# A joint opening of three weight groups in layer 1, and first token differences made in mid-layer

## The chip, the cores and the metric

The kernel runs on one core of one Trainium2 chip. The metric is the device time of one execution in microseconds (us). Three runs of the kernel before took 1093.97, 1093.69 and 1090.76 us: the median is 1093.69 us.

A core has a matrix engine (TensorE, PE in the profile), whose weight loads are listed apart (PEld), and three engines for elementwise work: VectorE (DVE), ScalarE (ACT) and GpSimd (POOL). SyncE (SP) issues the DMAs. Each engine works through its own queue in order, and semaphores make one wait for another.

## The reference

The reference is a block of two layers over 1024 latent tokens of width 1024. Layer 0 mixes tokens by a Fourier transform in half of its channels and by differential attention in the other half. Layer 1 is a short gated convolution. Only layer 1 matters here, and of it this is what is computed:

```python
h = rms_norm(x, g) * (1.0 + scale) + shift
bg, cg, xt, g = jnp.split(h @ odd_w_in, 4, axis=-1)      # 1024 x 4096
u = cg * xt
up = jnp.pad(u, ((0, 0), (1, 1), (0, 0)))
conv = sum(conv_w[t] * up[:, t:t + n] for t in range(3))
y = (bg * conv * jax.nn.silu(g)) @ odd_w_out             # 1024 x 1024
return x + gate * y
```

All is float32.

## The kernel before, in words

Features lie on the 128 partitions, tokens along the free axis, in two halves of 512 (NB). A float32 product is made of three matmuls of a faster 32-bit format: each operand is split into a high part (a cast on ACT) and a low part (the operand less its high part, a subtract on DVE or POOL), and high x high, high x low and low x high are added in PSUM.

**Seven products for eight.** Layer 1's two projections are done in 20 *groups*: 16 for the input projection (0 to 15) and 4 for the output projection (16 to 19). A group has two column tiles of 128 features, and its 2 x 2 blocks (token half by input half) are computed with seven products instead of eight, from sums and differences of blocks. A product (g, p), p = 1 to 7, is 4 quarters of 3 matmuls, each 128x128 by 128x512, in `quarters`. It needs a weight operand, made by `wop` and `wpart` from the raw tiles `wraw` of its group, and a token operand B[p] of four tiles (k = 0 to 3), each with a high and a low part. The token operands are shared by all groups of a projection: B[1] and B[2] are parts of the first token half, B[5], B[6], B[7] and B[4] are differences (t1, t2, t3, t4 in the code), and B[3] is a part of the second half. Each difference is formed from the one before it. The weight operand of p = 5 takes three or four elementwise steps on POOL (L634), the others none.

Products 1, 6, 7 and 4 of a group add into one PSUM bank, X, without starting anew. Between them ACT or DVE must read the bank, and the next product waits for that. Product 2 uses bank Z, products 5 and 3 use bank Y. `finish1` does the elementwise work behind each product of groups 0 to 15: even groups give u = cg * xt and end with the convolution (`conv`, two scalings on ACT and 12 taps on DVE, L1389, result in `vv`), odd groups give bg * silu(g) and are multiplied by `vv`; their results are listed in `ysd`. `finish2` does the output projection's.

**The opening of layer 1.** While layer 0's output projection of the second token half still runs (`out0(1, f)`), the first half is normalised and B[1] and B[2] are made. What needs the second half waits for its norm: token sums (`stats1`, small matmuls in mid-product), rs and dg on DVE with a power on POOL between, then a broadcast matmul (`ps_rows`), whose result `scaled` reads. TensorE does meanwhile the products that need the first half alone: (0,1), (0,2), (1,1), (1,2), with the token sums in the middle of (0,2) and the broadcast in the middle of (1,1). Then groups 0 and 1 go on together through p = 5, 6, 7, while B[5], B[6], B[7], B[4], B[3] are made just ahead of them, and (0,4), (0,3) close the opening. Group 2 begins behind it. In this part the order of every engine's queue is the program's (a manual schedule of PE, DVE, ACT and POOL). The low parts of B alternate between DVE and POOL, as do those of the weights.

**The middle**, up to group 14, fixes TensorE's order alone; a planner with costs of its own orders the other engines. Weights are prepared five products ahead (LEAD). Weight operands go round six buffers, in the pools `wp` (4) and `w2` (2); raw tiles have two buffers in each pool, and a group's are reloaded when product 3 of the group two before it has been prepared.

**The end**, from (14,1) on, is again in program order on all four engines. Here a weight's high part is cast at one product and its low part made behind the next (the lists `rests` and `due`). The token operands of the output projection are made from `ysd` by `bop`, at the places listed in `hooks`: a subtract where B is a difference, a cast, and a low part that is held back by one step (`lows`).

## Time and profile before

| | |
|---|---|
| median of three runs | 1093.69 us |
| the profiled execution | 1093.98 us |
| its span | 1092.2 us |
| TensorE busy | 1039.5 us (95%) |
| DVE busy | 753.0 us (69%) |
| ACT busy | 481.9 us (44%) |
| POOL busy | 466.8 us (43%) |
| mean granted TensorE clock | 0.981 |

A row of the timeline gives the start and the duration of an instruction in us, its engine, the line of the kernel, what it writes and reads, and in brackets how long the engine had been idle and what ended that. "xN" stands for N instructions merged. The durations of matmuls overlap: it is the distance of their starts that tells their rate. The granted clock is 1.00 where TensorE runs at full speed.

### The profile page before, as it was taken

Reading aid. Unit: us, or ns where it says so; the run is one execution under the profiler, and the core shown is the slowest. Engines: PE = TensorE matmul, PEld = TensorE weight load, DVE = VectorE, ACT = ScalarE, POOL = GpSimd, SP = SyncE. Lnnn points to the kernel's source line nnn. Section 1 sums busy time; section 2 is a strip of 40 time slices with the busy share of each in tenths; the row PEclk is TensorE's granted clock in tenths of the full one; section 3 lists DMA queues with packets and bytes.
Section 4 is the critical chain, followed back from the end, with each engine's and each line's share of the span. In section 5 each row is a group of like instructions: output and inputs, shape, how many; then the busy total and the mean of one; then the engine's idle time right before and its main releaser. Section 6 shows DMA issues by size and latency. Waiting matters only on the chain.

```text
span 1092.2 us, 14128 instructions
## 1 busy us (share of the span) xinstructions
PE 1039.5 (95%) x5128; PEld 847.3 (78%) x5128; DVE 753.0 (69%) x1093; ACT 481.9 (44%) x876; POOL 466.8 (43%) x398
## 2 busy tenths in 40 slices
PE   6989999999999899999999998899999999998998
PEld 3667888878877698999888886578888888786786
DVE  4599956958786388888853287986545645578953
ACT  4453333313345377777753363633333333344420
POOL 1257115620445147766575445655344354402041
PEclk8999999999999999999999999999999999999999
DMA  9823895353112978161006450121111211202431
GB/s 337 329 97 113 260 367 214 110 166 115 59 44 78 244 185 189 38 163 57 11 20 210 166 189 34 38 77 40 59 58 39 77 40 58 77 20 97 143 126 59
DMA packets 61381, 131.12 MB, mean 120 GB/s; under 512 B 5248, under 2 KB 30208, under 8 KB 58112
## 3 DMA queue, kind: packets, MB, share of 16 engines
q1 hardware_dynamic: 60240, 125.64, 36.7%
q0 software_dynamic: 1072, 4.59, 1.2%
q8 instruction: 40, 0.66, 0.2%
q14 instruction: 29, 0.24, 0.1%
HBM read 105.57 MB, written 24.64 MB: 119 GB/s over the span
## 4 chain that ended last, share of the span: by engine, by line
PE 64%; DVE 20%; POOL 5%; ACT 4%; issue 3%; DMA 3%; SPq 0%; ACTq 0%; POOLq 0%; DVEq 0%
PE psX L657 6%; PE psX L659 6%; PE psX L658 6%; PE ps_av L1075 5%; PE ps_tok L284 3%; PE ps_tok L285 3%; PE ps_tok L286 3%; PE psY L657 3%; PE psY L659 3%; PE psY L658 3%; PE S L1025 3%; PE S L1026 2%; DVE nm L1030 2%; PE ps_t L1065 2%; PE ps_feat L1128 2%
## 5 line engine op out<-in xcount | busy, mean ns | idle before, releaser
L284 PE MATMUL ps_tok<-whi,hhi 128*128 128x512 f32 x288 | 118.5, 412 | 2.5 <-ACT hhi L393 1.5
L285 PE MATMUL ps_tok<-whi,hlo 128*128 128x512 f32 x288 | 115.3, 400 | 3.6 <-DVE hlo L397 3.5
L286 PE MATMUL ps_tok<-wlo,hhi 128*128 128x512 f32 x288 | 114.6, 398 | 0.0
L61 ACT CAST wop<-wraw 128x512 fp32r<-128x512 f32 x118 | 72.5, 620 | 93.4 <-PE ps_feat L1130 27.6
L1030 DVE TENSOR_REDUCE nm<-S 128x1 f32<-128x1280 f32 x64 | 95.2, 1487 | 20.5 <-PE S L1026 18.4
L634 POOL TENSOR_TENSOR s<-wraw 128x512 f32<-128x512 f32 x20 | 27.9, 1395 | 185.3 <-DMA wraw<-in_wodd_dram 118.1
L62 POOL TENSOR_TENSOR wop<-wraw,wop 128x512 fp32r<-128x512 f32 x60 | 83.1, 1388 | 51.5 <-ACT wop L61 51.5
L1041 ACT ACTIVATE p<-S,nm 128x1280 f32<-128x1280 f32 x64 | 85.1, 1330 | 43.2 <-DVE nm L1030 39.4
L657 PE MATMUL psX<-B,wop 128*128 128x512 f32 x240 | 96.7, 403 | 7.5 <-ACT c L1363 3.5
L658 PE MATMUL psX<-B,wop 128*128 128x512 f32 x240 | 96.5, 402 | 1.5 <-POOL B L1510 1.0
L659 PE MATMUL psX<-B,wop 128*128 128x512 f32 x240 | 96.1, 401 | 1.8 <-DVE wop L1310 1.3
L1075 PE MATMUL ps_av<-v,aT 128*128 128x128 f32 x640 | 76.8, 275 | 0.0
L1075 PEld LDWEIGHTS ps_av<-v,aT 128*128 128x128 f32 x640 | 74.2, 192 | 0.2
L285 PEld LDWEIGHTS ps_tok<-whi,hlo 128*128 128x128 f32 x288 | 55.5, 193 | 16.9 <-DVE hlo L397 6.0
L659 PE MATMUL psY<-B,wop 128*128 128x512 f32 x160 | 64.3, 402 | 4.1 <-DVE wop L1310 4.1
L284 PEld LDWEIGHTS ps_tok<-whi,hhi 128*128 128x128 f32 x288 | 55.6, 193 | 16.2 <-issue 2.1
L1052 POOL TENSOR_TENSOR p<-p,cc 128x256 f32<-128x256 f32 x32 | 40.3, 1259 | 63.8 <-DVE cc L1049 44.6
L286 PEld LDWEIGHTS ps_tok<-wlo,hhi 128*128 128x128 f32 x288 | 55.4, 192 | 12.2 <-DVE wlo L172 0.2
L658 PE MATMUL psY<-B,wop 128*128 128x512 f32 x160 | 64.1, 401 | 0.6 <-POOL B L1510 0.3
L657 PE MATMUL psY<-B,wop 128*128 128x512 f32 x160 | 64.0, 400 | 0.0
L657 PEld LDWEIGHTS psX<-B,wop 128*128 128x128 f32 x240 | 45.7, 191 | 21.3 <-ACT c L1363 4.8
L658 PEld LDWEIGHTS psX<-B,wop 128*128 128x128 f32 x240 | 45.7, 191 | 14.3 <-POOL B L1510 2.4
(347 smaller groups left out, 2696.0 us busy)
## 6 DMA issues: line engine op xcount, KB each, us to landing
ada_raw<-in_ada_dram SPq DMA_DIRECT2D x24, 1024.0 KB, 7.6
wraw<-in_wodd_dram SPq DMA_DIRECT2D x32, 512.0 KB, 3.5
wraw<-in_wo_dram SPq DMA_DIRECT2D x24, 512.0 KB, 4.1
wraw<-in_wtok_dram SPq DMA_DIRECT2D x16, 512.0 KB, 5.1
arena<-kd SPq DMA_DIRECT2D x16, 320.0 KB, 9.3
kq<-kd SPq DMA_DIRECT2D x16, 320.0 KB, 10.1
xt<-in_xT_dram SPq DMA_DIRECT2D x16, 256.0 KB, 5.8
xr<-in_xT_dram SPq DMA_DIRECT2D x16, 256.0 KB, 4.0
```

The lines of the kernel that those rows point to most:

```text
L61: nc.scalar.copy(out=o[:, 0, :], in_=src)
L62: eng.tensor_tensor(out=o[:, 1, :], in0=src, in1=f32(o[:, 0, :]), op=ALU.subtract)
L284: nc.tensor.matmul(ps, lhsT=hh, rhs=whi, start=k == 0, stop=False)
L285: nc.tensor.matmul(ps, lhsT=hl, rhs=whi, start=False, stop=False)
L286: nc.tensor.matmul(ps, lhsT=hh, rhs=wlo, start=False, stop=k == KT - 1)
L657: nc.tensor.matmul(ps, lhsT=a, rhs=x[k][0], start=start and k == 0, stop=False, skip_group_check=not start)
L658: nc.tensor.matmul(ps, lhsT=a, rhs=x[k][1], start=False, stop=False, skip_group_check=not start)
L659: nc.tensor.matmul(ps, lhsT=b, rhs=x[k][0], start=False, stop=k == 3, skip_group_check=not start)
L1030: nc.vector.tensor_reduce(out=nm, in_=S[m][:, :NKEY], op=ALU.max, axis=AX.X, negate=True)
L1041: nc.scalar.activation(out=p, in_=S[m][:, :NKEY], func=AF.Exp, bias=tiles.pop((i, m, "nm")), accum_out=z)
L1052: nc.gpsimd.tensor_tensor(out=p1[:, ks], in0=p1[:, ks], in1=c.broadcast_to([P, POOLK]), op=ALU.mult)
L1075: nc.tensor.matmul(ps, lhsT=groups[i, k // 4][:, (k % 4) * P:(k % 4 + 1) * P], rhs=v[:, k * P:(k + 1) * P], start=k == 0, stop=k == NK - 1)
```

## The change

The opening takes group 2 in. Its order becomes (0,1), (0,2), (1,1), (1,2), (2,1), (2,2), then 5 for groups 0, 1, 2, then 6 and 7 for 0 and 1, then (0,4), (1,4), (0,3), (1,3), (2,6), (2,7), (2,4); group 3 follows. All low parts of token operands and weights in it are made on DVE. Weight preparation is cut into its cast and its low part (`later=True`), which are placed by hand; two steps of the weights for product 3 are deferred (`held`), and so are the copies behind (2,1) and (2,2), and the convolution of group 0 with what follows it for group 1 (`tails`, behind (2,6)).

The manual schedule begins one output tile of layer 0 earlier, and group 0's raw tiles are loaded at its third tile. Pools and buffers change places: the six weight buffers begin with `w2`; group 0's raw tiles lie in `w2`, group 1's in `wp`, group 2's in two of the four B3 buffers; two B3 tiles use buffers of `x1`, and the results of groups 11 and 13 use B3 buffers. (1,2)'s bank Z is a Y buffer, (2,5)'s bank Y a buffer of the small pool.

For the output projection's operands, `eop` takes the place of `bop`. The difference of B[5] is made for all four k at product (10,6) (`eop_early`) and lies in the second half of its y tile; the later differences are formed from it, and B[5] itself needs no subtract any more at its hook. In the end, the convolution of group 14 is emitted behind the weights' low parts that are due after (14,3), instead of ahead of them.

```diff
+    def eop_early(x, k):
+        q0, q1 = x[k]
+        if k not in early:
+            early[k] = None
+            nc.vector.tensor_tensor(out=q1, in0=q1, in1=q0, op=ALU.subtract)
...
+    def eop(p, x, k):
+        (q0, q1), (q2, q3) = x[k], x[k + 4] if p not in (1, 5) else (None, None)
+        t2 = q1 if early[k] is None else early[k]
+        src = {1: q0, 2: q2, 3: q3, 4: q2, 5: q1, 6: t2, 7: q0}[p]
+        if lows and lows[0][2] == k:
+            low()
+        if p == 6 and early[k] is None:
+            nc.vector.tensor_tensor(out=q1, in0=q3, in1=q1, op=ALU.subtract)
+        elif p in (4, 7):
+            nc.vector.tensor_tensor(out=src, in0=src, in1=t2, op=ALU.subtract)
+        low()
...
-    wpools[:] = [wp, wp, wp, wp, w2, w2]
+    wpools[:] = [w2, w2, wp, wp, wp, wp]
...
-                pool = (wp, w2)[g % 2]
-                t = pool.tile([P, KT * P], F32, name="wraw", bufs=2)
+                if g == 2:
+                    t = hB.tile([P, KT * P], F32, name="wraw", tag="B3", bufs=4)
+                else:
+                    t = (w2, wp)[(g + (g > 2)) % 2].tile([P, KT * P], F32, name="wraw", bufs=2)
...
-            if gated:
+            def last():
+                if not gated:
+                    return conv(ct, ubuf[ct % 2])
+                if g == 1:
+                    nc.vector.tensor_mul(out=h0, in0=h0, in1=vv[:, 0:NB])
                 nc.vector.tensor_mul(out=h1, in0=h1, in1=vv[:, NB:T])
                 ysd.append(us[g])
-            else:
-                conv(ct, ubuf[ct % 2])
+            if g in (0, 1, 14):
+                return last
+            last()
...
+            if half == 1 and f == 2:
+                wload(0)
             if half == 1 and f == KT - 2:
-                wload(0)
                 wload(1)
+                man.__exit__(None, None, None)
+                man = tc.manual_schedule(engines=MANUAL)
+                man.__enter__()
...
+            if half == 1 and f == KT - 2:
+                wop(0, 1, nc.vector)
+                wop(0, 2, nc.vector)
             if half == 1 and f == KT - 1:
-                for q in order[:5]:
-                    wop(*q)
...
+                wop(1, 1, nc.vector)
+                wop(0, 5, nc.vector)
...
-    wop(1, 5)
+    wload(2)
+    wop(1, 2, nc.vector)
...
     product(0, 1)
-    wop(0, 6)
-    product(0, 2, (2, stats_mid))
-    wop(1, 6, G)
+    wop(1, 5, V, held=held)
+    product(0, 2, (1, stats_mid))
+    w21 = wop(2, 1, V, True)
+    w22 = wop(2, 2, V, True)
     product(1, 1, (2, rows_mid))
...
+    fin2 = [product(2, p, later=True) for p in (1, 2)]
+    scaled(3), t1(2), t1(3), lo(5, 2, V), lo(5, 3, V)
+    fin12()
+    w25()
     product(0, 5)
...
     product(1, 5)
-    wop(0, 7, G)
+    product(2, 5)
+    t3(0), w16(), t3(1), lo(7, 0, V), t3(2), lo(7, 1, V), t3(3), lo(7, 2, V)
+    w07 = wop(0, 7, V, True)
+    lo(7, 3, V)
     product(0, 6)
+    t4(0), w07(), t4(1), lo(4, 0, V)
+    w17 = wop(1, 7, V, True)
     product(1, 6)
...
+    tails = [product(0, 3)]
+    wop(2, 4, V)
+    tails.append(product(1, 3))
+    wop(3, 1, V)
+    product(2, 6)
+    for f in tails:
+        f()
...
+        for k in {(10, 6): range(4)}.get((g, p), ()):
+            eop_early(ysd, k)
+        tail = product(g, p)
         for f in due:
             f()
+        if tail:
+            tail()
         for q, k0, k1 in hooks.get((g, p), ()):
             for k in range(k0, k1):
-                bop(q, ysd, k)
+                eop(q, ysd, k)
```

## The prediction

> **What bounds the kernel now.** I read the page's shares first, then a table of stretches, then TensorE's own timeline around the idle it shows.

> ```profile
> span 1092.2 us, 14128 instructions
> PE 1039.5 (95%) x5128; PEld 847.3 (78%) x5128; DVE 753.0 (69%) x1093; ACT 481.9 (44%) x876; POOL 466.8 (43%) x398
> ...
> 661.00:736.00 75.00, 63.22 (x246) 46.61 (x245) 66.31 (x77) 33.99 (x59) 45.84 (x31) 0.93 0.13 43
> 800.00:952.00 152.00, 152.00 (x653) 122.12 (x652) 81.96 (x134) 55.12 (x92) 63.63 (x46) 1.00 0.17 56
> 952.00:985.00 33.00, 32.79 (x141) 26.02 (x141) 21.34 (x34) 15.47 (x28) 3.87 (x3) 1.00 0.15 48
> 986.00:1028.00 42.00, 35.63 (x137) 26.96 (x135) 40.05 (x64) 19.05 (x34) 8.62 (x6) 0.92 0.26 83
> ```

> The stretch rows give length, then busy time of PE, weight loads, DVE, ACT, POOL, then the granted clock. The middle of layer 1 is pure TensorE: 152.00 of 152 us. Nothing can be won there. Time is lost in the opening of layer 1 (661 to 736) and in the end (986 to 1028); in both DVE is nearly full (66.31 of 75 and 40.05 of 42), so TensorE waits for DVE's queue, directly or through ACT.

> ```profile
> 660.40 0.39 PE L1128 MATMUL ps_feat<-yh,wop 128*128 128x512 f32 x1
> 660.63 0.40 PE L1129 MATMUL ps_feat<-yl,wop 128*128 128x512 f32 x1
> ...
> 661.10 0.40 PE L657 MATMUL psX<-arena,wop 128*128 128x512 f32 x1
> 665.30 0.28 PE L209 MATMUL ps_ss<-ones,x1ss 128*128 128x1 f32 x2
> 667.00 0.48 PE L657 MATMUL psZ<-arena,wop 128*128 128x512 f32 x1
> 673.71 1.44 PE L228 MATMUL ps_r<-dg,ones 128*128 128x512 f32 x2 [3.67 <-DVE dg L220]
> 675.38 0.63 PE L658 MATMUL psX<-arena,wop 128*128 128x512 f32 x1
> 705.64 0.79 PE L657 MATMUL psX<-B,wop 128*128 128x512 f32 x1 [2.46 <-ACT c L1363]
> 706.23 0.63 PE L658 MATMUL psX<-B,wop 128*128 128x512 f32 x1
> 706.66 0.63 PE L659 MATMUL psX<-B,wop 128*128 128x512 f32 x1
> 732.25 0.67 PE L657 MATMUL psX<-B,wop 128*128 128x512 f32 x1 [2.65 <-ACT u L1360]
> 736.70 0.40 PE L657 MATMUL psX<-arena,wop 128*128 128x512 f32 x1
> ```

> Matmuls start 0.2333 us apart (660.40, 660.63), so a product of 12 takes 2.80 us; after a long wait they start 0.43 apart (706.23, 706.66). Product (0,1) starts at 661.10, the twentieth product at 736.70: 75.60 us for 19 products. These need 19 x 2.80 = 53.2, the token sums take 1.7 (665.30 to 667.00), the two broadcast matmuls about 1.2 (673.71 to 675.38 less one matmul). **19.5 us of the opening is loss**: the three waits quoted, the half-speed rows after each, and many waits under 1 us.

> **The change, part by part.** The order of engine work in the opening is by hand, so I added each engine's instructions in the order of the new code. The prices:

> ```profile
> 1017.09 1.29 DVE L1270 TENSOR_TENSOR y<-y 128x512 f32<-128x512 f32 x2
> 675.19 1.41 DVE L1499 SCALAR_TENSOR_TENSOR x<-x,sc,ps_r 128x512 f32<-128x512 f32 x2 [0.94 <-PE ps_r L228]
> L1510 DVE TENSOR_TENSOR B<-x,B 128x512 fp32r<-128x512 f32 x11 | 10.8, 996 | 0.8 <-ACT B L1506 0.7
> L1510 POOL TENSOR_TENSOR B<-x,B 128x512 fp32r<-128x512 f32 x9 | 13.2, 1466 | 16.7 <-ACT B L1506 16.7
> 705.48 2.18 ACT L1506 CAST B<-x 128x512 fp32r<-128x512 f32 x4
> 668.87 1.29 POOL L634 TENSOR_TENSOR wraw<-wraw 128x512 f32<-128x512 f32 x1
> 668.93 1.77 DVE L62 TENSOR_TENSOR wop<-wraw,wop 128x512 fp32r<-128x512 f32 x1 [1.30 <-ACT wop L61]
> 670.63 0.15 DVE L216 TENSOR_SCALAR rs<-ps_ss 128x4 f32<-128x4 f32 x1
> 671.91 1.75 DVE L220 TENSOR_TENSOR dg<-cst,rs 128x512 f32<-128x512 f32 x1 [1.13 <-POOL rs L218]
> ```

> Two tensor_tensor take 1.29 us, so DVE issues one per 0.60 us; two scalar_tensor_tensor take 1.41, 0.66 each; four casts 2.18, 0.52 each. Beside a POOL subtract a DVE one takes 1.77, until the POOL one is over, and the B subtracts average 996 ns. The new opening puts the POOL subtracts on DVE: 0.60 added to DVE for 1.3 to 1.5 taken off POOL and off DVE's waits.

> *First wait (3.67).* The token sums were in by 667.0, but DVE reached rs at 670.63, behind the weight subtract that ended at 670.70, and dg took 1.75 beside POOL. In the new order weights (0,1), (0,2), (1,1), (0,5), (1,2) come earlier, since group 0's raw tiles are loaded first:

> ```profile
> 582.60 2.18 SPq L1294 DMA_DIRECT2D wraw<-in_wodd_dram  x2
> 649.83 0.39 SPq L1294 DMA_DIRECT2D wraw<-in_wodd_dram  x1
> 652.78 0.33 SPq L1294 DMA_DIRECT2D wraw<-in_wodd_dram  x1
> DMA to landing us min/median/max: 3.3/3.7/9.1
> ```

> The early pair (582.60) is now group 0's, the late one group 1's, landing at 653.5 and 656.5, while (1,1) is wanted at 668. Group 2's pair waits for memory that layer 0's last product frees (661.1), passes the last x1d store on SP and lands near 668; (2,1) is wanted at 674.9. So ahead of rs stands only (1,5), whose cast follows the table load and the copy of (0,1): subtract at about 666.8, rs 667.5, POOL's pow 1.0, dg 668.7 to 669.4. TensorE, with the sums after one quarter of (0,2), asks at 669.7. The wait is **0**, at most 1.

> *The operands.* From rows to the first token operand TensorE now has (1,2), (2,1), (2,2) to do instead of (1,2). Demand against supply, with no loss on TensorE:
> - (0,5) at 680.5. DVE from 670.9: 4 scalings and 4 differences, 5.3, 4 subtracts 2.4: 678.6, with some 1 us for three POOL steps of (2,5) 679.6. No wait.
> - (0,6) at 688.9, after three products instead of two. DVE: 2.6 + 11 x 0.60 = 9.2: 688.8. Only the last quarter is wanted that late; no wait.
> - (0,7) at 694.5, after two. Its X bank must be copied by ACT first, and the copy stands behind the cast of the fourth B7 tile and that of its weight. The fourth difference is the seventh instruction on DVE from some 689.2 (0.4 of waits for ACT): 4 x 0.66 + 3 x 0.60, done near 694; two casts and the copy (0.52, 0.52, 0.6) end at 695.7, and the weight's subtract 0.4 too late after it: **1.7 lost**.
> - (1,7), wanted at 694.5 + 1.7 + 2.8 + 0.5 = 699.5: its weight is the eighth instruction on DVE after 695.5, 700.3: **0.8 lost**.
> - (0,4), (1,4), (0,3), (1,3): DVE 4.2, then 5.4 of weights, deferred differences and bank sums, against 11.2 of TensorE: no wait.
> - (2,6), (2,7), (2,4) stand in one X bank back to back, so each waits for ACT's copy (about 0.84): **1.7 lost**. The convolution of group 0 comes behind (2,6) on DVE, when (1,3) is finished; so the 2.65 wait, which stood behind it, goes.

> That is 4.2, and 0.5 for port waits not placed. Two allowances. DVE is the pace for 30 us: were each instruction 0.03 us longer, the same addition gives 2.6 us more; I take half, 1.3. And the half clock:

> The rows after 705.64 and 732.25 show that 2.46 us of wait was enough for a stretch of eight matmuls 0.43 apart, 8 x 0.194 = 1.55 us; 0.94 us was not (1082.42, quoted below with the next start, 0.31 later). The 1.7 at (0,7) lies between: bounds 0 and 1.55, I take 0.8.

> [...]

> New loss 4.2 + 0.5 + 1.3 + 0.8 = 6.8; **the opening gains 12.7**. Bounds: 8 (DVE 10% slower throughout) to 15.

> *The middle.* Four subtracts, 2.4 us, are added on DVE at (10,6); DVE is busy 81.96 of 152 us there. Cost 0; uncovered 2.4. The buffers move (group 2's raw tiles and later two y tiles in B3 slots, two B3 tiles in x1 slots), with the same number of slots in use.

> *The end.*

> ```profile
> 1001.10 4.40 DVE L1389 SCALAR_TENSOR_TENSOR vv<-u,small,vv 128x256 f32<-128x256 f32 x12
> 1005.42 0.69 DVE L1310 TENSOR_TENSOR wop<-s,wop 128x512 fp32r<-128x512 f32 x1
> ...
> 1001.46 0.39 PE L657 MATMUL psY<-B,wop 128*128 128x512 f32 x1
> 1006.16 0.79 PE L659 MATMUL psY<-B,wop 128*128 128x512 f32 x1 [4.07 <-DVE wop L1310]
> 1021.01 0.50 PE L659 MATMUL psX<-B,wop 128*128 128x512 f32 x1 [0.60 <-DVE wop L1310]
> 1024.68 0.50 PE L659 MATMUL psZ<-arena,wop 128*128 128x512 f32 x1 [0.60 <-DVE wop L1310]
> 1028.49 0.50 PE L659 MATMUL psX<-B,wop 128*128 128x512 f32 x1 [0.75 <-DVE wop L1310]
> 1082.42 0.47 PE L657 MATMUL psX<-B,wop 128*128 128x512 f32 x1 [0.94 <-DVE out L1419]
> 1082.73 0.39 PE L658 MATMUL psX<-B,wop 128*128 128x512 f32 x1
> ```

> The 4.07 wait is (16,5)'s weight behind the 12 taps of group 14. Now that subtract goes first (0.60), the taps follow, and the subtract of (17,1) is late next: 1001.1 + 0.6 + 4.4 + 0.7 = 1006.8, wanted at 1001.46 + 2.80 + 0.47 = 1004.7. So 4.07 becomes 2.1, and the slow stretch may go. But the three later waits are on DVE as well, which idles only 1.95 of 42 us: TensorE will meet DVE's queue again. Four differences (2.4 us) leave DVE at 972 to 985, where it has 11.7 us idle: 0. Against it, the third and fourth B3 tile now take slots of y tiles whose last readers are the B3 subtracts just before, so cast and subtract go in turn, about 0.8. Between 0 and 2.7 I take **1.3**.

> Sum: 12.7 + 1.3 = 14.0. The profiled execution took 1093.98 us (span 1092.2 and 1.8 around it), 0.29 over the median of 1093.69: 1093.98 - 14.0 = 1080.0, as a median **1079.7**.

> **Rivals.** (a) *DVE becomes the opening's bound in full.* For it: 20 products' subtracts on one engine at its 996 ns, not 600. Against it: those 996 come from POOL work, of which only three steps are left in the stretch. With a mean of 0.70 a stall of 1.3 to 2.3 opens at (0,6), (0,7), (1,7), (0,3), with the slow clock after two: opening gain 5 to 8, total 7.5: 1086. (b) *Nothing is left to wait for*: DVE at 0.60 flat, no slow stretch, and the end gains its 2.7: 15 + 2.7, 1076. (c) *Slower: the middle loses its cover.* Beyond the opening only TensorE's order is by hand. Weights there are prepared from raw tiles reloaded when the last reader is done; with the opening done 15 us earlier, the loads of groups 3 and 4 start relatively later, and the planner may place later weights behind the convolution. It decides when a weight comes over 1.3 us late in each of the 11 groups 3 to 13 (11 x 1.3 = 14.3, the whole gain); at 2.65, the size of the wait quoted, it is 29, and the time 1079.7 + 29 = 1109. For it: the 2.65 wait stood behind a convolution too. Against it: 152.00 of 152 busy and DVE half idle. (d) *The opening's chain is only moved*: rs is no earlier, since (1,5)'s cast is late, and 3 us of the first wait and its slow stretch stay: 1084.

> **Chances.** The forecast 0.55 (1076 to 1083), (a) 0.17, (b) 0.10, (d) 0.10, (c) 0.05, nothing gained 0.03. The range from 1073 to 1088 leaves out (c), no gain and the worst of (a). A difference under about 0.3%, 3.3 us, can't be told from none here. Faster by more: 0.92; within: 0.03; slower: 0.05.

> **What would show it.** Right: ps_r without a wait over 1 us; (3,1) starting between 724 and 727 instead of 736.70 though one more product stands ahead of it; waits near 696 and 700 and two of 0.8 at (2,7), (2,4); DVE over 95% busy from 671 to 712; no POOL subtracts of B; the middle still without idle; in the end a wait of about 2 us at (17,1) and the three small ones kept. Wrong: a wait over 2 us at (0,6), idle in the middle, or an end that takes longer from (14,1) on than before.

## The result, and the profile after

Three runs of the changed kernel took 1080.34 to 1083.79 us, the median is **1081.78 us**; before it was 1093.69. The ratio on record is 0.9908 with a 95% interval of 0.9883 to 0.9933 (the two medians alone give 0.989): faster, with the whole interval below 1. The medians lie 11.9 us apart, 2.1 less than the 14.0 forecast; the profiled executions, 1093.98 and 1083.79 us, lie 10.2 apart.

The page's first lines and the table of stretches of the kernel after (length, busy time of PE, weight loads, DVE, ACT, POOL, granted clock, DMA share, GB/s):

```profile
span 1081.8 us, 14124 instructions
PE 1033.8 (96%) x5128; PEld 843.5 (78%) x5128; DVE 755.7 (70%) x1112; ACT 480.7 (44%) x876; POOL 436.4 (40%) x379
...
660.50:727.00 66.50, 62.42 (x259) 48.63 (x258) 60.55 (x89) 34.79 (x61) 15.02 (x11) 0.95 0.12 39
671.00:712.00 41.00, 39.49 (x163) 30.95 (x162) 40.25 (x65) 24.51 (x43) 1.42 (x1) 0.96 0.13 40
800.00:939.00 139.00, 139.00 (x598) 111.77 (x597) 77.78 (x127) 51.50 (x86) 59.12 (x42) 1.00 0.17 56
974.00:1018.00 44.00, 35.85 (x136) 26.75 (x135) 41.36 (x64) 17.45 (x31) 7.67 (x6) 0.92 0.29 96
```

In the opening (660.50 to 727.00) TensorE is busy 62.42 of 66.50 us, where it was 63.22 of 75. POOL is nearly empty from 671 to 712 (one instruction), and DVE nearly full (40.25 of 41). The middle is pure TensorE as before. The end (974 to 1018) has DVE nearly full, as before (41.36 of 44; it was 40.05 of 42).

To see where the time went, I take three lengths from the starts of matmuls: from the start of (0,1) to the start of the twenty-first product (then the opening is over in both kernels), from there to (14,1), and from (14,1) to the last matmul.

| us | opening, 20 products | middle | from (14,1) on |
|---|---|---|---|
| before | 78.40 | 212.80 | 135.56 |
| after | 66.64 | 212.67 | 137.36 |
| change | **-11.76** | -0.13 | **+1.80** |

So the opening gave nearly what was forecast (12.7), the middle nothing, as forecast, and the end lost 1.8 where 1.3 was to be won.

TensorE's timeline in the opening of the kernel after (start, duration, and in brackets the wait and what ended it):

```profile
669.30 1.02 PE L228 MATMUL ps_r<-dg,ones 128*128 128x512 f32 x2
...
695.43 0.50 PE L657 MATMUL psX<-B,wop 128*128 128x512 f32 x1 [1.31 <-ACT u L1396]
...
696.36 0.65 PE L659 MATMUL psX<-B,wop 128*128 128x512 f32 x1 [0.20 <-DVE wop L1342]
696.81 0.63 PE L657 MATMUL psX<-B,wop 128*128 128x512 f32 x1
697.24 0.63 PE L658 MATMUL psX<-B,wop 128*128 128x512 f32 x1
...
719.16 0.50 PE L657 MATMUL psX<-B,wop 128*128 128x512 f32 x1 [1.89 <-ACT u L1396]
724.26 0.50 PE L657 MATMUL psX<-B,wop 128*128 128x512 f32 x1 [0.68 <-ACT c L1399]
727.15 0.39 PE L657 MATMUL psX<-arena,wop 128*128 128x512 f32 x1
```

The broadcast (669.30) has no wait any more: 3.67 us are gone. (0,7) waits 1.31 and 0.20, and the slow rows follow it (0.43 between 696.81 and 697.24). Of the two waits for X banks late in the opening, one is 0.68, the other 1.89. ACT shows why:

```profile
716.45 0.63 ACT L1409 ACTIVATE y<-y 128x512 f32<-128x512 f32 x1 [6.32 <-DVE y L1407]
...
718.53 0.57 ACT L1396 COPY u<-psX 128x512 f32<-128x512 f32 x1
```

ACT stood idle for 6.32 us until DVE had y, then did group 1's SiLU and three weight casts 0.52 us apart, and only then the copy that frees (2,6)'s bank.

The end, all engines, of the kernel after:

```profile
988.45 0.69 DVE L1342 TENSOR_TENSOR wop<-s,wop 128x512 fp32r<-128x512 f32 x1
989.05 6.35 DVE L1431 SCALAR_TENSOR_TENSOR vv<-u,small,vv 128x256 f32<-128x256 f32 x12
989.37 1.32 POOL L634 TENSOR_TENSOR s<-wraw 128x512 f32<-128x512 f32 x1 [5.72 <-ACT vv L1428]
990.77 1.36 POOL L634 TENSOR_TENSOR wraw<-wraw 128x512 f32<-128x512 f32 x1
996.06 0.50 PE L659 MATMUL psX<-arena,wop 128*128 128x512 f32 x1 [3.82 <-DVE wop L1342]
...
1009.56 0.50 PE L659 MATMUL psX<-B,wop 128*128 128x512 f32 x1 [2.05 <-DVE wop L1342]
```

And the same POOL step in the kernel before, whose taps stood from 1001.10 to 1005.50:

```profile
1006.34 1.51 POOL L634 TENSOR_TENSOR s<-wraw 128x512 f32<-128x512 f32 x1 [10.03 <-DVE wop L1310]
```

Here is the step that I missed. The subtract `wop<-s` of (16,5) is the last reader of the buffer s, and POOL's next step writes s. Before, it stood behind the taps, so POOL waited for it (10.03 us of idle) and the taps ran alone in 4.40 us. Now it goes first (988.45), POOL starts beside the taps (989.37, 990.77), and the same twelve taps take 6.35 us. (The profile names ACT's scaling of `vv` as what ended POOL's 5.72 us, since that ended last. But POOL starts 0.23 us after the end of the subtract in both kernels, and in the kernel before the scaling had ended 4.4 us earlier.) The wait moved from (16,5) to (17,1) and shrank from 4.07 to 3.82 only.

### The profile page after: what moved, and what is told of

Its sections match the earlier page's. It is cut to its first block, busy times and chain, and to the rows that moved or that the text cites. A ratio compares the mean times of both kernels' runs of the same rounds, so it can differ in the third digit from the quotient of the medians.

```text
span 1081.8 us, 14124 instructions
## 1 busy us (share of the span) xinstructions
PE 1033.8 (96%) x5128; PEld 843.5 (78%) x5128; DVE 755.7 (70%) x1112; ACT 480.7 (44%) x876; POOL 436.4 (40%) x379
## 3 DMA queue, kind: packets, MB, share of 16 engines
q0 software_dynamic: 1072, 4.59, 1.2%
## 4 chain that ended last, share of the span: by engine, by line
PE 66%; DVE 19%; ACT 4%; POOL 4%; DMA 3%; issue 3%; SPq 0%; ACTq 0%; POOLq 0%; DVEq 0%
PE psX L659 7%; PE psX L657 7%; PE psX L658 6%; PE ps_av L1075 5%; PE ps_tok L284 3%; PE ps_tok L285 3%; PE ps_tok L286 3%; PE psY L657 3%; PE psY L658 3%; PE psY L659 3%; PE S L1025 3%; PE S L1026 3%; PE ps_t L1065 2%; DVE nm L1030 2%; PE ps_feat L1128 2%
## 5 line engine op out<-in xcount | busy, mean ns | idle before, releaser
L634 POOL TENSOR_TENSOR s<-wraw 128x512 f32<-128x512 f32 x20 | 26.9, 1347 | 215.5 <-DMA wraw<-in_wodd_dram 135.5
L657 PE MATMUL psX<-B,wop 128*128 128x512 f32 x240 | 97.1, 405 | 5.7 <-ACT u L1396 3.2
L61 ACT CAST wop<-wraw 128x512 fp32r<-128x512 f32 x106 | 65.3, 620 | 83.2 <-PE ps_feat L1130 19.4
L659 PE MATMUL psX<-B,wop 128*128 128x512 f32 x240 | 97.0, 404 | 3.1 <-DVE wop L1342 3.1
L658 PE MATMUL psX<-B,wop 128*128 128x512 f32 x240 | 96.2, 401 | 0.0
L62 POOL TENSOR_TENSOR wop<-wraw,wop 128x512 fp32r<-128x512 f32 x52 | 71.3, 1373 | 40.8 <-ACT wop L61 40.8
L659 PE MATMUL psY<-B,wop 128*128 128x512 f32 x160 | 63.1, 395 | 0.7 <-DVE wop L1342 0.7
L657 PE MATMUL psY<-B,wop 128*128 128x512 f32 x160 | 63.4, 396 | 0.0
L658 PE MATMUL psY<-B,wop 128*128 128x512 f32 x160 | 63.2, 395 | 0.0
L657 PEld LDWEIGHTS psX<-B,wop 128*128 128x128 f32 x240 | 45.8, 191 | 19.3 <-ACT u L1396 4.1
L659 PEld LDWEIGHTS psX<-B,wop 128*128 128x128 f32 x240 | 45.9, 191 | 15.8 <-DVE wop L1342 4.6
```

What stands on the lines that cost most here:

```text
L61: nc.scalar.copy(out=o[:, 0, :], in_=src)
L62: eng.tensor_tensor(out=o[:, 1, :], in0=src, in1=f32(o[:, 0, :]), op=ALU.subtract)
L657: nc.tensor.matmul(ps, lhsT=a, rhs=x[k][0], start=start and k == 0, stop=False, skip_group_check=not start)
L658: nc.tensor.matmul(ps, lhsT=a, rhs=x[k][1], start=False, stop=False, skip_group_check=not start)
L659: nc.tensor.matmul(ps, lhsT=b, rhs=x[k][0], start=False, stop=k == 3, skip_group_check=not start)
```

## The experiments

My theory at this point: the opening gained because operands and weights no longer wait in POOL's queue and the first norm is no longer late; the end lost because POOL's steps run beside the taps. The rivals: that one engine or one part made the whole gain of the opening; that the end is bound by VectorE whatever the order. All runs of a batch were compared with the kernel before on the same chip. The lengths are those of the table above, from one profile each.

| kernel | median us | ratio to before, 95% | opening | middle | end |
|---|---|---|---|---|---|
| open_only | 1081.65 | 0.9913 (0.9894 to 0.9932) | 66.50 | 212.65 | 136.13 |
| end_only | 1092.61 | 1.0017 (1.0002 to 1.0032) | 77.16 | 212.80 | 136.40 |
| conv_first | 1081.95 | 0.9920 (0.9902 to 0.9938) | 65.00 | 212.98 | 135.96 |
| pool_late | 1070.54 | 0.9818 (0.9795 to 0.9841) | 63.73 | 207.52 | 133.86 |
| pool_late0 | 1080.83 | 0.9901 (0.9883 to 0.9920) | 66.56 | 212.65 | 138.23 |
| pad_left | 1071.22 | 0.9812 (0.9792 to 0.9832) | 65.03 | 207.56 | 134.88 |
| pad_right | 1071.07 | 0.9812 (0.9793 to 0.9831) | 63.88 | 207.53 | 138.66 |
| before_pad | 1079.88 | 0.9896 (0.9878 to 0.9914) | 78.80 | 206.72 | 132.44 |
| lo_pool | 1084.10 | 0.9921 (0.9901 to 0.9941) | 67.25 | 212.98 | 139.23 |
| old_dve | 1090.33 | 0.9991 (0.9977 to 1.0005) | 74.76 | 212.80 | 136.09 |
| no_taps (the kernel after again, see below) | 1080.45 | 0.9907 (0.9890 to 0.9924) | 63.90 | 212.96 | 138.03 |
| best | 1068.83 | 0.9797 (0.9779 to 0.9815) | 63.73 | 207.50 | 134.11 |

### The opening alone, and the end alone

open_only is the new opening with the old end (old operands of the output projection, old place of group 14's convolution); end_only is the old opening with the new end:

```diff
  open_only, against after
-            if g in (0, 1, 14):
+            if g in (0, 1):
...
-        for k in {(10, 6): range(4)}.get((g, p), ()):
-            eop_early(ysd, k)
...
-                eop(q, ysd, k)
+                bop(q, ysd, k)
```

```diff
  end_only, against before
+        for k in {(10, 6): range(4)}.get((g, p), ()):
+            eop_early(ysd, k)
-        product(g, p)
+        tail = product(g, p)
...
+        if tail:
+            tail()
...
-                bop(q, ysd, k)
+                eop(q, ysd, k)
```

> The new opening alone: the end is that of before (first differences made in the end, convolution of group 14 ahead of the weights' low parts that are due), the new places of the y and B3 tiles stay. Theory (the opening gains 11.8 us, the new end costs 1.8): the time from (14,1) to the last matmul falls from 137.4 to about 136 (135.6 as before, and some 0.5 for B3 tiles that wait for y tiles), the 12 taps take 4.4 us instead of 6.35, and the kernel takes about 1080.3. Rival (the new end is even, and the 1.8 us are the accident of one profile): 1081 to 1082.5, not told from the full change.

> The kernel before with the new end alone: first differences in mid-layer, convolution of group 14 behind the due low parts; opening and buffers as before. Theory: the taps of group 14 run beside two POOL steps of group 17 and take about 6.3 us, (17,1) waits near 3.8 us where (16,5) waited 4.07, and the kernel is no faster: 1093.7 to 1095.5. Rival (the forecast): the taps keep 4.4 us, the wait halves to 2.1, 1092.4.

The opening alone gives the whole gain: 1081.65 us, ratio 0.9913. Its end takes 136.13 us and its taps 4.40, as the theory said; its time is the rival's, and can't be told from the full change. The end alone gains nothing; its ratio 1.0017 lies just above 1 with its whole interval. In end_only the taps stretch beside POOL as in the kernel after, and the wait comes at (17,1). Its timeline:

```profile
996.90 6.35 DVE L1421 SCALAR_TENSOR_TENSOR vv<-u,small,vv 128x256 f32<-128x256 f32 x12
997.21 1.31 POOL L634 TENSOR_TENSOR s<-wraw 128x512 f32<-128x512 f32 x1 [5.71 <-ACT vv L1418]
...
1003.90 0.59 PE L659 MATMUL psX<-arena,wop 128*128 128x512 f32 x1 [3.81 <-DVE wop L1340]
```

So the fault of the end does not come from the opening ahead of it. The expected times of end_only went by 1093.69 us for the kernel before; in its batch that kernel took 1090.68.

### The convolution ahead of the low parts again

```diff
  conv_first, against after
-            if g in (0, 1, 14):
+            if g in (0, 1):
```

> The full change with the convolution of group 14 ahead of the due low parts again, as before; the first differences stay in mid-layer. Theory: taps 4.4 us, (16,5) waits about 4.1 us, end 136 us, 1080.5. Rival (putting the low part of (16,5) first does gain what the forecast said): the end gets longer, 138 or more, and the kernel takes 1083.

The wait is back at (16,5), with the length that it had before. The timeline of conv_first:

```profile
992.15 0.80 PE L659 MATMUL psY<-B,wop 128*128 128x512 f32 x1 [4.09 <-DVE wop L1342]
```

The end takes 135.96 us, and the median is 1081.95: the order of taps and subtracts can't be told in the time. Nor can the early differences be seen there: with them, and the old order, the end is 0.4 longer than before (135.56). In the profiles the order does show: the four with the convolution ahead (before, old_dve, open_only, conv_first) have ends of 135.56 to 136.13 us, mean 135.9; the four with it behind and POOL not held (after, no_taps, lo_pool, end_only) have 136.40 to 139.23, mean 137.8.

### POOL's steps held behind the taps

Twice. pool_late writes the small operation that holds POOL into a new constant, pool_late0 into a buffer that is there already; the number that it writes is used by nobody.

```diff
  pool_late, against after
+            if g == 14:
+                late14 = const.tile([P, 1], F32, name="late14")
+                nc.gpsimd.tensor_tensor(out=late14, in0=vv[:, T - 1:T], in1=mhalf[:, 0:1], op=ALU.mult)
  pool_late0, against after
+            if g == 14:
+                nc.gpsimd.tensor_tensor(out=ones_dv, in0=vv[:, T - 1:T], in1=mhalf[:, 0:1], op=ALU.mult)
```

> The full change, with one small POOL instruction added that reads the last column of the convolution's result, so that POOL's steps for (17,5) come behind the 12 taps and not beside them. Theory (the taps are slowed by these steps): taps 4.4 us again, the wait at (17,1) falls from 3.82 to about 1.9, without or with a shorter half-speed stretch, the end falls from 137.4 to 135 or so, and the kernel takes 1080 or less. Rival (DVE's queue bounds the end whatever waits first): the taps get shorter but the later waits at (17,5) or (16,6) grow by as much, the end stays at 137, 1081 to 1082.

> GpSimd's two steps of (17,5) held behind the convolution of group 14 by a small GpSimd operation that reads the convolution's result, written into a buffer that is there already: no address moves. Theory that the late release of these steps' buffer was what kept the GpSimd steps off the convolution: twelve taps 4.4 us instead of 6.35, wait at (17,1) about 1.9 us instead of 3.8, spacing of the matmuls 0.233, end 1 to 2 us shorter, 1080 to 1081 us. Rival, the end is bound by VectorE whatever the order: the taps shorten but later waits grow by as much, end 137.4 us, 1081.8 us.

pool_late took 1070.54 us, 11 us less than the kernel after, and nobody had expected that. Its middle is 207.52 us long instead of 212.67, though nothing is changed there: this gain has another cause, for which see the next experiments. pool_late0, which adds no buffer, took 1080.83. Its end:

```profile
987.21 4.39 DVE L1431 SCALAR_TENSOR_TENSOR vv<-u,small,vv 128x256 f32<-128x256 f32 x12
...
992.21 1.29 POOL L634 TENSOR_TENSOR s<-wraw 128x512 f32<-128x512 f32 x1
992.25 0.50 PE L659 MATMUL psX<-arena,wop 128*128 128x512 f32 x1 [1.84 <-DVE wop L1342]
...
995.28 1.26 POOL L634 TENSOR_TENSOR wraw<-s,wraw 128x512 f32<-128x512 f32 x1
995.34 1.75 DVE L1410 TENSOR_TENSOR y<-y,c 128x512 f32<-128x512 f32 x1 [0.70 <-ACT y L1409]
...
998.48 0.61 PE L659 MATMUL psY<-B,wop 128*128 128x512 f32 x1 [3.16 <-DVE wop L1342]
```

With POOL held off, the taps take 4.39 us and (17,1) waits 1.84: the 4.40 and the 2.1 of the prediction. This shows what stretched the taps. But POOL's steps then run beside the next DVE work (a product of tensors of 1.75 us at 995.34), and the following subtract is 3.16 us late. The end takes 138.23 us, no less than 137.36. The rival is right in its outcome: the wait only moves.

### The twelve taps left out, which did not come about

```diff
  no_taps, against after
+        if ct == 14:
+            return
```

> The kernel after with the twelve VectorE steps of group 14's convolution left out (the centre tap on ScalarE stays), so 4.4 us of VectorE work, 6.35 us as measured beside GpSimd, is missing from the end. Theory that VectorE bounds the stretch from (14,1) to (20,1) whatever the order: the wait at (17,1) goes and the end shortens by 4 to 7 us, 130.5 to 133.5 us, 1075 to 1078 us. Rival, the later waits hang on chains of ScalarE and VectorE and on transfers and not on VectorE's load: only the wait at (17,1) goes, another takes its place, end 136 to 137 us, 1080 to 1082 us.

The condition names column tile 14, but the convolution's tiles are counted from 0 to 7 (group 14 is tile 7), so it never holds: the taps are there, nothing is left out, and the run is the kernel after once more (1080.45 us). What the end would take with less DVE work was not tried, so it stays open whether DVE's load bounds it. As a repeat the run has its use. Its waits at (0,7) and (1,7) and the taps, from its timeline:

```profile
694.21 0.50 PE L657 MATMUL psX<-B,wop 128*128 128x512 f32 x1 [1.32 <-ACT u L1396]
...
695.14 0.50 PE L659 MATMUL psX<-B,wop 128*128 128x512 f32 x1 [0.19 <-DVE wop L1342]
695.48 0.39 PE L657 MATMUL psX<-B,wop 128*128 128x512 f32 x1
695.71 0.39 PE L658 MATMUL psX<-B,wop 128*128 128x512 f32 x1
...
698.75 0.50 PE L659 MATMUL psX<-B,wop 128*128 128x512 f32 x1 [0.56 <-DVE wop L1342]
...
985.32 6.34 DVE L1431 SCALAR_TENSOR_TENSOR vv<-u,small,vv 128x256 f32<-128x256 f32 x12
```

The waits at (0,7), 1.32 and 0.19, are those of the kernel after (1.31 and 0.20), yet full speed follows: 0.23 from 695.48 to 695.71, against 0.43 there. The opening takes 63.90 instead of 66.64 us with the same code: the kernel after has two slow stretches in it, behind (0,7) and behind the wait of 1.89, and the repeat has none. Two profiles of the same opening can therefore lie 2.7 us apart. Five profiles with this opening (after, open_only, conv_first, pool_late0, no_taps) lie at 63.90 to 66.64, mean 65.7; two of the old one (before, end_only) at 78.40 and 77.16, mean 77.8: **12.1 us** between the means.

### Which part of the opening made the gain

lo_pool gives nine of the low parts of the new opening back to POOL. old_dve makes on DVE the low parts of the old opening that its hand-written order gives to POOL; three low parts of weights that the planner places late in it stay on POOL (705.42, 719.26 and 724.53 in its trace).

```diff
  lo_pool, against after (so for nine of them, of B5, B6, B7, B4 and B3)
-    scaled(0), scaled(1), t1(0), scaled(2), t1(1), lo(5, 0, V), lo(5, 1, V)
+    scaled(0), scaled(1), t1(0), scaled(2), t1(1), lo(5, 0, V), lo(5, 1, G)
...
  old_dve, against before (so for all low parts of B, and those of weights placed by hand)
-    wop(1, 6, G)
+    wop(1, 6, V)
...
-    t3(0), t3(1), lo(7, 0, V), lo(7, 1, G)
+    t3(0), t3(1), lo(7, 0, V), lo(7, 1, V)
```

> The kernel after with nine of the opening's low parts (two each of B5, B6, B7 and B3, one of B4) formed on GpSimd again, as in the kernel before. Theory that the opening gained because no low part and no weight waits in GpSimd's queue: the wait at (0,7) grows from 1.31 to 2.8 us and a second one of 0.8 us comes behind it, first opening products to (3,1) 69 to 70 us instead of 66.6, 1084 to 1085 us. Rival, the first differences made in mid-layer and the shorter chain are the whole gain and the engine of the low parts does not matter: 66 to 67 us, 1081 to 1082 us; with VectorE less loaded it could even gain 1 us.

> The kernel before with all the opening's low parts of token operands and weights formed on VectorE instead of partly on GpSimd; the first differences are still made inside the opening. Theory that the GpSimd queue was one part of the loss of 19.5 us and the late chain of operands the other: opening to (3,1) 74 to 75 us instead of 78.4, after is 66.6, so a third of the gain; 1087 us. Rival, the queue was the whole of it: about 67 us, 1080 us. Rival, VectorE was the bound already: 78 us or more, 1090 to 1094 us.

The groups of the B subtracts (engine, operation, count: least, median and greatest duration in ns, first and last start) in lo_pool:

```profile
L1561 DVE TENSOR_TENSOR B<-x,B x11: 677/680/1787, 672.8 to 705.3; 128x512 fp32r<-128x512 f32 x11
L1561 POOL TENSOR_TENSOR B<-x,B x9: 1292/1386/1686, 673.6 to 703.3; 128x512 fp32r<-128x512 f32 x9
```

and in the kernel after:

```profile
L1561 DVE TENSOR_TENSOR B<-x,B x20: 679/690/694, 674.5 to 705.4; 128x512 fp32r<-128x512 f32 x20
```

The waits of lo_pool:

```profile
694.25 0.51 PE L657 MATMUL psX<-B,wop 128*128 128x512 f32 x1 [1.88 <-ACT u L1396]
...
709.00 0.50 PE L659 MATMUL psY<-B,wop 128*128 128x512 f32 x1 [0.54 <-DVE wop L1342]
```

On DVE alone no subtract of B is stretched (694 ns at most). With POOL beside it one is (1787), as are some other DVE instructions (1.78 us at 690.76, 1.68 at 693.74), the wait at (0,7) grows from 1.31 to 1.88, and a new one of 0.54 comes later (709.00). The theory had expected 2.8 and 0.8, and an opening of 69 to 70 us. It takes 67.25, above all five of the others but only 1.5 above their mean. The median of 1084.10 is the one that the theory named, but it can't be told from 1081.78, and the end of this profile is the longest of all (139.23). So the engine of these nine subtracts is worth some 1.5 us by one profile, less than the 2.7 by which two profiles of one opening differ.

The waits that old_dve keeps:

```profile
670.46 1.13 PE L228 MATMUL ps_r<-dg,ones 128*128 128x512 f32 x2 [2.21 <-DVE dg L220]
701.79 0.50 PE L657 MATMUL psX<-B,wop 128*128 128x512 f32 x1 [3.48 <-ACT c L1363]
...
728.36 0.50 PE L657 MATMUL psX<-B,wop 128*128 128x512 f32 x1 [2.35 <-ACT u L1360]
```

Its opening takes 74.76 us, as expected (74 to 75): 3.6 less than before in the profile. The time was not as expected (1087): the median, 1090.33, is only 1.3 lower, which this measurement can't tell from nothing. The three long waits stay: the broadcast (2.21), (0,7) (3.48), and the one late in the opening (2.35). In the kernel after, with its new order, they are 0, 1.31 and 1.89, and group 2's products stand in between. Most of the gain is this order: lo_pool, which has it with nine subtracts on POOL, has an opening of 67.25 us against the 78.40 of before. The engine is the smaller part. Which part of the order does it, the products of group 2, the earlier weights or the later copies, no run takes apart.

### The address

Between pool_late and pool_late0 only one thing differs for TensorE: the new constant of 4 bytes moves buffers. By the addresses in the built kernels before and after, the weights' buffers (wp, w2) start at a multiple of 64 bytes, and those of the token operands (hB, and the pool of arena) 32 bytes past one. The new constant shifts the pools on the left, the weights among them, by 32 bytes: then both start at 32 past a multiple of 64. Three kernels take this apart:

```diff
  pad_left, against after, and before_pad, against before
+    pad = const.tile([P, 1], F32, name="pad")
+    nc.vector.memset(pad, 0.0)
  pad_right, against after: the right-hand pools shifted by 32 bytes instead, so both at a multiple of 64
+    pad = opn("padr", "right").tile([P, 8], F32, name="pad")
+    nc.vector.memset(pad, 0.0)
```

> The kernel after with one more 4-byte constant a partition, which shifts the buffers of the weights, of x1 and h and of layer 0's first tokens by 32 bytes against the right-hand buffers; GpSimd's steps of (17,5) stay where they were. If the address is what made the run with late GpSimd faster (theory of the address): matmuls of the token products 0.227 us apart instead of 0.233, 1070 to 1073 us. If it was the late GpSimd steps or the chip's state: spacing 0.233, 1081 to 1082 us.

> The kernel after with 32 bytes put ahead of the right-hand buffers instead, so that token operands and weights both start at a multiple of 64 bytes. If what counts is that both operands of a matmul have the same offset modulo 64 bytes: spacing 0.227, 1070 to 1073 us, as with the pad on the left. If what counts is that the weights lie at 32 modulo 64 (theory of the weight address): spacing 0.233, 1081 to 1082 us.

> The kernel before with the same 4-byte constant. Theory of the address: matmul spacing 0.227, 10 to 11 us faster, about 1080 us. Rival (the address matters only together with the new order): 1090 to 1091 us, no change.

The stretch from 800 to 939, all TensorE, has 598 matmuls in the kernel after (its row stands above, the number in brackets), and as many in the kernel before. In pad_left, pad_right and before_pad:

```profile
800.00:939.00 139.00, 138.78 (x613) 114.63 (x612) 78.33 (x128) 51.77 (x87) 58.42 (x42) 1.00 0.17 57
```

```profile
800.00:939.00 139.00, 138.78 (x612) 114.68 (x611) 77.58 (x127) 51.02 (x87) 57.36 (x41) 1.00 0.17 57
```

```profile
800.00:939.00 139.00, 139.00 (x615) 115.16 (x614) 79.21 (x130) 52.66 (x89) 59.01 (x42) 1.00 0.17 57
```

In the same 139 us TensorE does 612 to 615 matmuls instead of 598, at the same granted clock of 1.00. The count takes in matmuls cut by the edges; the 76 products of the middle, 12 matmuls each, give the distance: 206.72 us in before_pad and 212.80 before, 0.2267 us a matmul instead of 0.2333. It does not matter on which side the pad lies (613 matmuls and 612), so it is not the weights' own address: **here matmuls whose two operands start at equal offsets modulo 64 bytes follow each other in 0.2267 us, those with 32 bytes between in 0.2333**. Other distances were not tried, so that 64 is the modulus is not shown. The pad takes some 10 us off the kernel after (1071.22 and 1071.07, against 1081.78 in another batch and 1080.83 for pool_late0 in their own) and 11.3 off the kernel before (1079.88 against 1091.22 in its batch): about as much as the whole change. Why the offset counts, these runs do not show.

The kernel before has both cases in one profile. Two unbroken rows of layer 0's matmuls, the first with both operands at a multiple of 64, the second with 32 bytes between (first and last matmul of each):

```profile
265.52 0.39 PE L822 MATMUL ps_feat<-hhi,whi 128*128 128x512 f32 x1
...
276.18 0.40 PE L824 MATMUL ps_feat<-hhi,wlo 128*128 128x512 f32 x1
...
580.76 0.39 PE L1128 MATMUL ps_feat<-yfo,wop 128*128 128x512 f32 x1
...
619.02 0.39 PE L1130 MATMUL ps_feat<-yh,wop 128*128 128x512 f32 x1
```

The first row is 48 matmuls, 47 distances of 0.2267 us; the second 165, 164 distances of 0.2333. A short row gained less. In the kernel after, the two B3 tiles that use buffers of `x1` lie at a multiple of 64, as the weights do. A product 3 of groups 3 to 12, with six equal pairs of twelve, takes 2.783 us there against 2.800 for the others (medians of the distances of starts), where 0.2267 for the six would give 2.76.

### The best of it

pad_left, with the convolution where it was before, and the outputs of groups 9 and 11 in place of 11 and 13 in the buffers of B3:

```diff
  best, against after
+    pad = const.tile([P, 1], F32, name="pad")
+    nc.vector.memset(pad, 0.0)
...
-                us[g] = halves(hB.tile([P, T], F32, name="y", tag="B3", bufs=4) if g in (11, 13) else
+                us[g] = halves(hB.tile([P, T], F32, name="y", tag="B3", bufs=4) if g in (9, 11) else
...
-            if g in (0, 1, 14):
+            if g in (0, 1):
```

> The kernel after with the 4-byte constant that shifts the left-hand buffers by 32 bytes, the convolution of group 14 put ahead of the last low parts again, as in the kernel before, and the outputs of groups 9 and 11 in place of 11 and 13 in the buffers of B3, so that the last low parts of B3 do not wait for their high parts. If the gains add: 1071.2 - 1.4 (end 135.96 instead of 137.36) - 0.8 (the chain over B3), 1068 to 1070 us. Rival, the end is bound by VectorE and its waits only move: 1070 to 1072 us.

1068.83 us, ratio 0.9797 (0.9779 to 0.9815): the fastest of all, within the 1068 to 1070 expected. The intervals of best and pad_left overlap, so that the two edits of the end add anything isn't shown. The B3 subtracts do run without waits for ACT between them now; in the kernel after, casts and subtracts waited for each other there (0.69 us before the subtract at 1016.47). The timeline of best:

```profile
1000.85 2.67 DVE L1261 TENSOR_TENSOR B<-y,B 128x512 fp32r<-128x512 f32 x4
```

## Why the prediction was right, and where it was wrong

The time (1081.78 against 1079.7), the sign and the likeliest case held. In part this is luck of the median: by the two profiled executions the gain is 10.2 us of the 14.0 forecast, 0.9 short in the opening and 3.1 in the end. Of its own signs, (3,1) starts at 727.15, just behind the 724 to 727 named, and one sign of being wrong came true: the end takes longer from (14,1) on than before. By its own steps:

- **First wait, 3.67 to 0.** Right: 669.30 has no wait.
- **(0,7), 1.7 lost.** Measured 1.31 + 0.20. Right in place, releaser and size.
- **(1,7), 0.8 lost.** In the kernel after there is none; in the repeat without slow rows TensorE waits 0.56 there (698.75). The five profiles agree: no wait in the two with slow rows behind (0,7), 0.55 to 0.56 in the three without. The slow rows gave DVE the time. Right within 0.3.
- **X bank late in the opening, 2 x 0.84.** One was 0.68, the other 1.89. The second was mis-sized: the addition left out what stands ahead of ACT's copy, a SiLU that waits for DVE and three weight casts (716.45 to 718.53). In the five profiles with this opening it was 1.19 to 2.29.
- **Half clock, 0.8 between 0 and 1.55.** Each bound came true at (0,7): 1.55 in the kernel after, 0 in its repeat, with the same wait ahead. The sum had no term for a second slow stretch; the kernel after has one behind the 1.89 wait (granted clock 0.50 from 720.44 to 723.85).
- **Port waits, 0.5.** No run shows a port, or this term by itself. What the traces show of DVE beside POOL is 1787 ns for one subtract of B in lo_pool; in the kernel after none took over 694.
- **DVE's pace, allowance 1.3; rival (a).** No subtract of B took over 694 ns, and two in a row take 1.29 (699.83), so they are 0.60 us apart, as priced; 40.25 of 41 us are busy. Rival (a) needed a mean of 0.70 us between them and does not hold.
- **Opening, 12.7.** Measured 11.8 by the two first profiles, 12.1 by the means.
- **Middle, 0.** Right: 139.00 of 139 busy, 212.67 against 212.80 us. Rival (c) has nothing for it. Rival (d) falls with the first wait, rival (b) with the new waits.
- **End, +1.3.** Wrong in sign in the profiles: 1.8 longer, by the two first profiles and by the means of four each (135.9 and 137.8). The step that failed is "the taps follow" at 4.4 us, so that "4.07 becomes 2.1". It took the 4.40 of a profile in which POOL stood idle for 10.03 us, and did not ask what POOL waited for. That was the very subtract which the change moves ahead of the taps. Measured 6.35 for the taps and 3.82 for the wait; with POOL held, 4.39 and 1.84. Two terms beside it: four differences off DVE brought nothing (135.96 with them in the old order, 135.56 before), and the warning in the same part, that TensorE will meet DVE's queue again, held in every version tried (ends of 135.56 to 139.23 us where no buffer was moved).

In the medians the end's loss is at the limit of what can be told: end_only is slower than before by 0.02 to 0.32%, while after and open_only differ by nothing (0.9908 and 0.9913).

## What to carry to other kernels

Before a reader of a buffer is moved ahead, look up who writes that buffer next: the writer is released with it, and if it is POOL beside DVE, the work now behind it can get slower (here 6.35 us instead of 4.39). A duration taken from a profile is one beside the neighbour that the engine had there (these taps took 4.40 us with POOL idle). And compare the start addresses of a matmul's two operands: 32 bytes of padding were worth as much here (10 to 11 us) as a rebuilt opening (11.8).

## What the runs showed of the hardware

**Equal offsets.** 0.2267 us a matmul in before_pad, against 0.2333 before (128x128 by 128x512, four-byte operands, in long rows), when both operands start at the same offset modulo 64 bytes instead of 32 bytes apart, told above.

**The granted clock changed on a grid of 3.413 us.** Stretches of the kernel before (the first two rows) and of the kernel after; the granted clock is the third number from the end:

```profile
674.39:677.81 3.42, 3.42 (x9) 2.34 (x8) 2.62 (x4) 0.06 (x1) 0.00 (x0) 0.50 0.02 5
705.11:708.53 3.42, 2.89 (x7) 2.31 (x8) 3.42 (x5) 3.42 (x7) 2.29 (x3) 0.50 0.50 153
```

```profile
693.13:696.54 3.41, 1.90 (x8) 0.94 (x7) 3.33 (x6) 2.24 (x4) 0.00 (x0) 1.00 0.00 0
696.54:699.95 3.41, 3.41 (x9) 2.64 (x10) 3.41 (x7) 2.74 (x6) 0.00 (x0) 0.50 0.00 0
```
